# Trunk of a streaming encoder: sums of the first norm from two layouts of x, a 512-column first MLP product, and a written order for the last stage

## The chip, the cores and the metric

The kernel runs on one core of a Trainium2 chip. The time is that of one execution on the device, in microseconds, the median of several runs. The core has a matrix engine (PE; its weight loads are shown apart as PEld), a vector engine (DVE), a scalar engine (ACT), a third compute engine (POOL, also called GpSimd), and queues of DMA transfers, most of which are issued by SP. Each engine works through its own list of instructions in order and waits on semaphores where an operand comes from another engine.

## The reference, cut to what matters

With one layer (`DEPTH` is 1) the trunk is one Conformer convolution module, one squared-ReLU MLP and a final norm, on x of 512 tokens and 2048 channels in float32:

```python
h = rmsnorm(x, norm1_g)
u = h @ w_in + b_in                        # 2048 -> 2 * 2048
val, gate = split(u)
u = val * sigmoid(gate)
u = causal_dwconv(u, dw) + dw_b            # 31 taps for each channel
u = silu(layernorm(u, ln_g, ln_b))
x = x + u @ w_out + b_out
h = rmsnorm(x, norm2_g)
x = x + square(relu(h @ mlp_w1)) @ mlp_w2  # 2048 -> 8192 -> 2048
return rmsnorm(x, final_g)                 # rmsnorm: y * rsqrt(mean(y*y) + 1e-6) * g
```

## The kernel before, in words

Everything but the ends of the kernel lies channel-major: a tile holds 128 channels on the partitions and 512 tokens in the free dimension. To keep float32 precision each operand of a large product is split into a high part and a low rest, and each product is made of three matmuls (`mm3`, lines 377 to 382): weights-high by data-high, weights-high by data-low, weights-low by data-high. The high parts of weights are made on ACT (line 139, 237, 242), the low rests on POOL or DVE (line 140, 238, 243). A `Stream` object makes weight chunks some chunks ahead of their use (`AHEAD`), in four pairs of buffers.

The stages, in order of time:

- **Front.** 16 tiles of x arrive by DMA (`xt`). Each is multiplied by the norm's gain and split (`split_scaled`, ACT line 373, DVE line 374). Its squares are taken on ACT or DVE (string `SQ_X`) and added into two sums over channel tiles, `acc1` on POOL and `acc2` on DVE (string `ADD_X`, line 499); line 522 adds the two. `col_sums` (line 360) turns them into one number for each token by matmuls against ones, `inv_sqrt` makes the factor `r`, and `spread` (line 366) lays it out over the partitions as `row1`. The factor is applied only after the projection, so the matmuls of the input projection do not wait for it. The string `LO_W0` says which engine makes the low rests of the first eight weight chunks (v is DVE, g is POOL).
- **Input projection and convolution.** For each of 16 channel tiles j, 96 matmuls of 512 columns (`in_tile`) fill two PSUM banks. `gate(j)` and `glu(j)` make the gated value (DVE lines 411, 413, 421, ACT line 415), and `conv(j)` adds 31 taps, 24 or 25 of them on DVE (line 463), the others by ACT and POOL (lines 442, 452). The last tile is done in two halves, with some taps on PE by diagonal matrices (`diags`, line 566).
- **Layer norm and output projection** (line 758).
- **First MLP product.** The 64 tiles of 128 hidden channels are taken as 32 pairs. A pair's product is done by a Strassen-like scheme of seven products on halves (`FIRST`): halves of the input channels, of the pair, and of the tokens, so that each product has 256 columns (`HT`). A product is eight sets of `mm3`. Data tiles `y` hold high and low part side by side, 256 columns each. Four PSUM banks collect the products (`BANK`); P1, then P6, P7 and P4 accumulate in the same bank, and after each of these products the partial sum is read out into `four` (lines 1083, 1085, 1087). `Squares.step` then applies ReLU and square to the pair before, splits it and stores it to DRAM.
- **Second MLP product**, again in seven products, for all but the last two pairs of hidden tiles.
- **Last stage.** The last pair of hidden tiles is multiplied plainly for each block b of 128 tokens, in four pieces of 512 output columns (the last piece of the last block in two of 256). Each piece is added to the residual on DVE (`add`, line 1154), squared and summed on ACT (line 1230), multiplied by the final gain on POOL (line 1232; the block's last piece on DVE, line 1240), and, once all the block's sums are there, scaled by the norm's factor on ACT or DVE (lines 1247, 1249) and sent out by SP.

Inside `with tc.manual_schedule()` the instructions stand in each engine's list as the code writes them; elsewhere a scheduler of the tile library places them. Front, layer norm and both MLP products are written by hand; the pieces of the last stage are placed by the scheduler, all but the block of code around the norm's factor.

Of the kernel before, what the change touches and what calls it, by code (L numbers as in the profile page):

```python
# [12 lines left out]
F32 = mybir.dt.float32  # L13
# [5 lines left out]
P = 128  # L19
T = 512  # L20
# [26 lines left out]
ADD_X = "ggvgvgggggvgggvg"  # L47
SQ_X = "avaavaavaavaavaa"
LO_W0 = "vvvvgvgg"
# [34 lines left out]
def trunk(ctx: ExitStack, tc: tile.TileContext, xT, vec, fg, w_in, w_out, w1s, w2s, w2b, out):  # L84
# [272 lines left out]
    def col_sums(dst, acc):  # L357

        for b in range(NTOK):
            nc.tensor.matmul(out=dst[:, b : b + 1], lhsT=acc[:, b * P : (b + 1) * P], rhs=ones, start=True, stop=True)  # L360

# [129 lines left out]
    sums_on = [(nc.gpsimd, acc1) if c == "g" else (nc.vector, acc2) for c in ADD_X]  # L491
    with tc.manual_schedule():
        begun = set()
        pending = None

        def add(item):
            eng, acc, sq = item
            if sq is not acc:
                eng.tensor_tensor(out=acc, in0=acc, in1=sq, op=ALU.add)

        stream.AHEAD = 0
        for k in range(NT):
            nc.sync.dma_start(out=xt[k], in_=xT[:, k, :])
            if k % 4 == 1 and k > 1:
                stream.emit()
# [5 lines left out]
            eng, acc = sums_on[k]  # L511
            first = id(acc) not in begun
            begun.add(id(acc))
            sq = acc if first else early.tile([P, T], F32, tag="t", name="sq", bufs=4)
            if SQ_X[k] == "a":
                nc.scalar.activation(out=sq, in_=xt[k], func=AF.Square)
            else:
                nc.vector.tensor_tensor(out=sq, in0=xt[k], in1=xt[k], op=ALU.mult)
            pending = (eng, acc, sq)
        add(pending)  # L520
        if len(begun) > 1:
            nc.vector.tensor_tensor(out=acc1, in0=acc1, in1=acc2, op=ALU.add)
# [3 lines left out]
        for k in range(NT):  # L526
            in_tile(0, k, w0[k // 4])
            if k % 4 == 3:
                stream.emit()
        w1 = [chunk() for _ in range(4)]  # L530
        pvg[1] = (bank(), bank())
        st = bank("ax")
        col_sums(st, acc1)
        ms = tmp.tile([P, NTOK], F32, tag="st", name="ms")
        nc.vector.tensor_scalar(out=ms, in0=st[:, :NTOK], scalar1=1.0 / D, scalar2=None, op0=ALU.mult)
        r = inv_sqrt(ms, eps_rms, RMS_EPS, NTOK)
# [758 lines left out]
```

## Time and profile before

| | before |
|---|---|
| median of 3 runs | 1876.59 us (1876.09 to 1877.53) |
| the profiled execution | 1875.1 us, span of its instructions 1873.3 us |
| busy share | PE 98%, PEld 87%, DVE 67%, ACT 62%, POOL 68% |
| mean granted TensorE clock | 0.993 of full |

The span is the time from the first to the last instruction of the profiled execution. A busy share counts time in which at least one instruction of the engine runs. Matmuls are pipelined: a row gives the time from start to modelled end of one, and the distance between the starts of two rows is what one costs.

### The profile page before, as it was taken

The page shows a single profiled execution, that of the slowest core. Times are in us where ns is not written, and L with a number is a line of the kernel's source. Part 1 is how long each engine was busy: PE and PEld are TensorE (multiplying, and loading weights), DVE is VectorE, ACT ScalarE, POOL GpSimd, SP SyncE. Part 2 cuts the span into 40 slices and gives each one's busy share as a digit, 9 for nine tenths or more (in the row PEclk, how much of TensorE's full clock was granted, in tenths as well). Part 3 has the DMA queues.
Part 4 walks back from the last instruction along what each step waited for, and adds up shares of the span by engine and source line. Part 5 has one row for each costly group of instructions (what it writes and reads, how often), then busy time and mean ns, then how long its engine had stood idle before and what let it go on. Part 6 is the DMA issues. An engine that isn't in the chain of part 4 may idle for free.

```text
span 1873.3 us, 29336 instructions
## 1 busy us (share of the span) xinstructions
PE 1827.9 (98%) x10860; PEld 1629.8 (87%) x10860; DVE 1254.7 (67%) x2001; ACT 1157.0 (62%) x1782; POOL 1271.5 (68%) x718
## 2 busy tenths in 40 slices
PE   6999999989999999999999999999999999999996
PEld 4888888879888999999999999998888888888875
DVE  8899999994338655555555555545666666665676
ACT  6444444456337666666666666647777777777774
POOL 6689999954432676776776776766666677566654
PEclk9999999999999999999999999999999999999998
DMA  5233333206333465565565565586557456474332
GB/s 204 95 102 100 104 114 111 80 1 214 113 113 128 154 219 190 180 218 192 179 216 196 179 215 193 178 309 239 214 196 283 159 222 247 174 280 186 137 133 90
DMA packets 91439, 320.99 MB, mean 171 GB/s; under 512 B 10144, under 2 KB 11808, under 8 KB 91296
## 3 DMA queue, kind: packets, MB, share of 16 engines
q1 hardware_dynamic: 70416, 257.71, 39.4%
q10 hardware_dynamic: 20880, 61.42, 8.2%
q8 instruction: 85, 1.39, 0.3%
q14 instruction: 58, 0.48, 0.1%
HBM read 254.60 MB, written 64.49 MB: 170 GB/s over the span
## 4 chain that ended last, share of the span: by engine, by line
PE 83%; DVE 12%; ACT 2%; issue 1%; DMA 1%; ACTq 0%; SPq 0%; POOL 0%; DVEq 0%; POOLq 0%
PE mm L380 25%; PE mm L381 25%; PE mm L382 25%; PE mm L758 7%; DVE ax L463 4%; DMA xt<-in_xT 1%; DVE xl L374 1%; DVE d L647 1%; DVE u L421 0%; DVE y L893 0%; DVE d L725 0%; DVE acc L1154 0%; DVE wl L140 0%; PE ax L901 0%; DVE xr L915 0%
## 5 line engine op out<-in xcount | busy, mean ns | idle before, releaser
L380 PE MATMUL mm<-y,wh 128*128 128x256 f32 x1792 | 508.7, 284 | 2.0 <-ACT x L912 1.1
L381 PE MATMUL mm<-y,wh 128*128 128x256 f32 x1792 | 508.3, 284 | 1.7 <-DVE y L893 1.7
L382 PE MATMUL mm<-y,wl 128*128 128x256 f32 x1792 | 508.2, 284 | 0.0
L238 POOL TENSOR_TENSOR wl<-b,wh 128x1024 fp32r<-128x1024 f32 x96 | 231.6, 2412 | 215.0 <-ACT wh L237 215.0
L380 PEld LDWEIGHTS mm<-y,wh 128*128 128x128 f32 x1792 | 345.1, 193 | 2.4 <-ACT x L912 1.3
L381 PEld LDWEIGHTS mm<-y,wh 128*128 128x128 f32 x1792 | 345.2, 193 | 1.9 <-DVE y L893 1.9
L214 DVE TENSOR_TENSOR wl<-b,ax 128x512 fp32r<-128x512 f32 x360 | 231.4, 684 | 171.7 <-ACT ax L213 127.0
L382 PEld LDWEIGHTS mm<-y,wl 128*128 128x128 f32 x1792 | 345.1, 193 | 0.0
L380 PE MATMUL mm<-wh,ah 128*128 128x512 f32 x840 | 326.9, 389 | 1.2 <-DVE acc L1154 1.2
L381 PE MATMUL mm<-wl,ah 128*128 128x512 f32 x840 | 326.8, 389 | 0.0
L382 PE MATMUL mm<-wh,al 128*128 128x512 f32 x840 | 326.8, 389 | 0.0
L187 POOL TENSOR_TENSOR b<-b,b 128x1024 f32<-128x1024 f32 x120 | 286.8, 2413 | 47.9 <-DVE wl L214 33.9
L207 ACT CAST wh<-b 128x1024 fp32r<-128x1024 f32 x210 | 221.3, 1054 | 151.5 <-PE mm L382 150.8
L140 POOL TENSOR_TENSOR wl<-raw,wh 128x1024 fp32r<-128x1024 f32 x85 | 206.8, 2452 | 103.1 <-ACT wh L139 103.0
L463 DVE SCALAR_TENSOR_TENSOR ax<-u,v,ax 128x512 f32<-128x512 f32 x327 | 218.1, 750 | 0.0
L380 PE MATMUL mm<-xh,wh 128*128 128x512 f32 (+1 forms) x544 | 207.1, 381 | 5.7 <-ACT wh L139 5.2
L381 PE MATMUL mm<-xl,wh 128*128 128x512 f32 (+1 forms) x544 | 207.7, 382 | 3.2 <-DVE xl L374 3.0
L382 PE MATMUL mm<-xh,wl 128*128 128x512 f32 (+1 forms) x544 | 206.6, 380 | 2.9 <-DVE wl L140 2.9
L213 ACT COPY ax<-wh 128x512 f32<-128x512 f32 x360 | 199.8, 588 | 5.7
L1154 DVE SCALAR_TENSOR_TENSOR acc<-mm,shift,acc 128x512 f32<-128x512 f32 (+1 forms) x241 | 169.6, 743 | 31.6 <-PE mm L382 31.6
L380 PEld LDWEIGHTS mm<-wh,ah 128*128 128x128 f32 x840 | 157.7, 188 | 34.7 <-ACT w2h L1205 1.6
L382 PEld LDWEIGHTS mm<-wh,al 128*128 128x128 f32 x840 | 157.7, 188 | 32.7
(216 smaller groups left out, 3047.3 us busy)
## 6 DMA issues: line engine op xcount, KB each, us to landing
b<-in_w1s SPq DMA_DIRECT2D x128, 512.0 KB, 4.6
b<-in_w2s SPq DMA_DIRECT2D x120, 512.0 KB, 6.7
raw<-in_w_in SPq DMA_DIRECT2D x63, 512.0 KB, 3.3
ah<-spill SPq DMA_DIRECT2D x26, 896.0 KB, 8.7
al<-spill SPq DMA_DIRECT2D x26, 896.0 KB, 10.3
raw<-in_w_out SPq DMA_DIRECT2D x32, 512.0 KB, 3.3
spill<-sh ACTq DMA_DIRECT2D x31, 512.0 KB, 7.2
spill<-sl ACTq DMA_DIRECT2D x31, 512.0 KB, 5.9
```

The costliest lines, as they stand in the source:

```text
L140: (nc.vector if sl.stop == cut else self.eng).tensor_tensor(out=lo[:, sl], in0=raw[:, sl], in1=hi[:, sl].bitcast(F32), op=ALU.subtract)
L187: nc.gpsimd.tensor_tensor(out=raw[to, hs], in0=raw[x, hs], in1=raw[y, hs], op=ALU.subtract)
L207: nc.scalar.copy(out=hi, in_=self.s)
L213: nc.scalar.copy(out=st, in_=hi[:, sl].bitcast(F32))
L214: nc.vector.tensor_tensor(out=lo[:, sl], in0=self.s[:, sl], in1=st, op=ALU.subtract)
L238: nc.gpsimd.tensor_tensor(out=lo, in0=raw[b], in1=hi.bitcast(F32), op=ALU.subtract)
L380: nc.tensor.matmul(out=ps, lhsT=wh, rhs=xh, start=first, stop=False, **how)
L381: nc.tensor.matmul(out=ps, lhsT=wh, rhs=xl, start=False, stop=False, **how)
L382: nc.tensor.matmul(out=ps, lhsT=wl, rhs=xh, start=False, stop=last, **how)
L463: nc.vector.scalar_tensor_tensor(out=o, in0=a, scalar=w, in1=c, op0=ALU.mult, op1=ALU.add)
L758: nc.tensor.matmul(out=ps[n][:, sl], lhsT=a[:, wsl], rhs=x[:, sl], start=first and a is wh and x is hi, stop=last and x is lo)
L1154: nc.vector.scalar_tensor_tensor(out=t, in0=ps, scalar=r2[:, b : b + 1], in1=t, op0=ALU.mult, op1=ALU.add)
```

## The change

The squares of channels 0 to 1023 are still taken from the channel-major tiles (all on ACT), and are added on DVE, in a PSUM bank, with no work on POOL. Those of channels 1024 to 2047 come from a second, token-major copy of that half of x (`x2d`, four tiles of 128 tokens by 1024 channels, four added DMA transfers of 512 KB): one ACT instruction squares a tile and adds along the free dimension, so that the result is already one number for each token. The sums by matmul are now issued after k = 13 of the first projection tile, `spread` after k = 2 of the second, and a sigmoid on a dummy follows the square root on ACT. Two more low rests of the first weight chunks change engine or place, and the twelve activations that make `diags` move to a place after the last full convolution.

In the first MLP product weights-high is multiplied by the whole data tile, high and low part in one matmul of 512 columns, and weights-low by the high part, 256 columns. The two halves of the bank are added while they are read out: one instruction takes the first half, one more on DVE adds the second.

In the last stage all is written in order: block b's square root factor and scaled outputs stand between the pieces of block b + 1, and the gain of a block's last piece moves to POOL, but for the last block.

```diff
-ADD_X = "ggvgvgggggvgggvg"
-SQ_X = "avaavaavaavaavaa"
-LO_W0 = "vvvvgvgg"
+STAT_AT = 13
+ROW_AT = 3
+SQ_AT = (10, 12, 14, 15)
+SQ_DVE = ()
+LO_W0 = "vvvvvvgg"
...
+        def squares(b):
+            t = big.tile([P, 2 * T], F32, tag="rb", name="xs")
+            nc.sync.dma_start(out=t, in_=x2d[b])
...
+                nc.scalar.activation(out=t, in_=t, func=AF.Square, accum_out=ms[:, b : b + 1])
...
+            elif k % 4 == 3:
+                stream.emit()
             if pending:
-                add(pending)
...
+                nc.vector.tensor_tensor(out=pending[0], in0=sq_acc, in1=pending[1], op=ALU.add)
+                pending = None
+            if k == 0:
+                nc.scalar.activation(out=sq_acc, in_=xt[k], func=AF.Square)
+            elif k < NT // 2:
+                sq = early.tile([P, T], F32, tag="t", name="sq", bufs=4)
                 nc.scalar.activation(out=sq, in_=xt[k], func=AF.Square)
...
+                pending = (acc1 if k == NT // 2 - 1 else sq_acc, sq)
+            if k in SQ_AT:
+                squares(SQ_AT.index(k))
+        stream.emit()
...
+            if k == STAT_AT:
+                st = bank("ax")
+                for b in range(NTOK):
+                    nc.tensor.matmul(out=st[:, b : b + 1], lhsT=acc1[:, b * P : (b + 1) * P], rhs=ones, start=True, stop=True)
...
+        nc.scalar.activation(out=root0, in_=eps_rms, func=AF.Sigmoid)
...
-                nc.scalar.activation(out=self.a[:, HT:], in_=self.a[:, HT:], func=AF.Relu)
+                nc.scalar.activation(out=self.a, in_=self.a, func=AF.Relu)
...
                 for p in range(8):
                     t = y[p, product]
-                    sl = slice(p * P, (p + 1) * P)
-                    mm3(x, tuple(h[:, sl] for h in w), (t[:, :HT], t[:, HT:]), product in OPENS and p == 0, p == 7, skip_group_check=True)
+                    wh, wl = (h[:, p * P : (p + 1) * P] for h in w)
+                    nc.tensor.matmul(out=x, lhsT=wh, rhs=t, start=product in OPENS and p == 0, stop=p == 7, skip_group_check=True)
+                    nc.tensor.matmul(out=x[:, :HT], lhsT=wl, rhs=t[:, :HT], start=False, stop=p == 7, skip_group_check=True)
...
-                if product in ("P1", "P5", "P6"):
-                    nc.scalar.copy(out=to, in_=x)
-                elif product == "P4":
-                    nc.scalar.activation(out=to, in_=x, func=AF.Relu)
+                if product in ("P2", "P7", "P3"):
+                    nc.vector.tensor_tensor(out=to, in0=x[:, :HT], in1=to, op=ALU.add)
                 else:
-                    nc.vector.tensor_tensor(out=to, in0=x, in1=to, op=ALU.add)
+                    nc.scalar.copy(out=to, in_=x[:, :HT])
+                nc.vector.tensor_tensor(out=to, in0=x[:, HT:], in1=to, op=ALU.add)
...
+    with tc.manual_schedule():
+        before = None
+        for b in range(NTOK):
+            row = Row(b)
+            for i, cs in enumerate(row.cols):
+                row.piece(i, cs)
+                if before and i == 0:
+                    before.factor()
+                    before.scale(3, False)
+                    before.scale(2, False)
+                elif before and i < 3:
+                    before.scale(2 - i, True)
+                if i < len(row.cols) - 1:
+                    row.gain(i, nc.gpsimd)
+            row.total()
+            row.gain(i, nc.gpsimd if b < NTOK - 1 else nc.vector)
+            before = row
+        before.factor()
+        for i in (4, 0, 3, 1, 2):
+            before.scale(i, i < 2)
```

`Row.piece` holds a piece's matmuls, its `add` and its square; `total` the sum and square root, `factor` the three small DVE instructions behind it, `scale` the scaled output and its DMA.

**Engine PE, first MLP product, before** (`mm` is the PSUM bank, `y` the data tile with high and low part, `wh` and `wl` the high and low weights; the end of two sets and the start of a third):

```order
L380 MATMUL mm_5318<-y_4390,wh_8710 128x256
L381 MATMUL mm_5318<-y_4390,wh_8710 128x256
L382 MATMUL mm_5318<-y_4390,wl_8711 128x256
L380 MATMUL mm_5318<-y_4423,wh_8710 128x256
L381 MATMUL mm_5318<-y_4423,wh_8710 128x256
L382 MATMUL mm_5318<-y_4423,wl_8711 128x256
L380 MATMUL mm_5318<-y_4698,wh_8710 128x256
L381 MATMUL mm_5318<-y_4698,wh_8710 128x256
```

The same engine and stage in the change, the last sets of one product and the first of the next:

```order
L1082 MATMUL mm_5309<-y_5350,wh_7612 128x512
L1083 MATMUL mm_5309<-y_5350,wl_7613 128x256
L1082 MATMUL mm_5309<-y_5394,wh_7612 128x512
L1083 MATMUL mm_5309<-y_5394,wl_7613 128x256
L1082 MATMUL mm_5311<-y_4383,wh_7645 128x512
L1083 MATMUL mm_5311<-y_4383,wl_7646 128x256
```

Three matmuls of 256 columns on a data tile have become one of 512 and one of 256.

**Engine DVE, end of the front, before** (`xl` is the low part of an x tile, `sq` squares, `wl` low weights, `ms` the mean of squares; in brackets the engines or transfers waited for):

```order
L374 SCALAR_TENSOR_TENSOR xl_259<-xt13_122,v_91,xh_258 128x512 [waits DMAHW2_49,Activation_49]
L518 TENSOR_TENSOR sq_263<-xt13_122 128x512 [waits Pool_49]
L374 SCALAR_TENSOR_TENSOR xl_267<-xt14_123,v_91,xh_266 128x512 [waits DMAHW4_49,Activation_49]
L374 SCALAR_TENSOR_TENSOR xl_275<-xt15_124,v_91,xh_274 128x512 [waits DMAHW5_49,Activation_49]
L499 TENSOR_TENSOR acc2_108<-acc2_108,sq_271 128x512 [waits DVE_49]
L522 TENSOR_TENSOR acc1_107<-acc1_107,acc2_108 128x512 [waits DVE_49,Pool_49]
L140 TENSOR_TENSOR wl_341<-raw_342,wh_340 128x1024 [waits DMAHW0_49,PE_49,Activation_49]
L535 TENSOR_SCALAR ms_413<-ax_408 128x4 [waits PE_49]
```

The same engine and place in the change (`mq` is the sum of both parts of the mean of squares):

```order
L371 SCALAR_TENSOR_TENSOR xl_255<-xt13_122,v_91,xh_254 128x512 [waits DMAHW5_49,Activation_49]
L371 SCALAR_TENSOR_TENSOR xl_260<-xt14_123,v_91,xh_259 128x512 [waits DMAHW6_49,Activation_49]
L371 SCALAR_TENSOR_TENSOR xl_268<-xt15_124,v_91,xh_267 128x512 [waits DMAHW0_49,Activation_49]
L142 TENSOR_TENSOR wl_272<-raw_273,wh_271 128x1024 [waits DMAHW1_49,PE_49,Activation_49]
L142 TENSOR_TENSOR wl_281<-raw_282,wh_280 128x1024 [waits DMAHW3_49,PE_49,Activation_49]
L533 TENSOR_TENSOR mq_390<-ax_373,ms_132 128x4 [waits PE_49]
L534 TENSOR_SCALAR mq_390<-mq_390 128x4 [waits DVE_49]
```

The squares, the adds and the joint sum are gone from this end of the list, one more low rest stands before the sums, and no wait on POOL is left.

**Engine ACT, last block of tokens, before** (`acc` and two digits is the piece of block and column, `sq` its squares, `r4` the factor of a block; rows with `r4` scale an output):

```order
L1230 ACTIVATE sq_18790,ss_18781<-acc30_13394 128x512
L1247 ACTIVATE acc21_13434<-acc21_13434,r4_18762 128x512
L1247 ACTIVATE acc20_13385<-acc20_13385,r4_18762 128x512
L1230 ACTIVATE sq_18801,ss_18781<-acc31_13443 128x512
L1230 ACTIVATE sq_18812,ss_18781<-acc32_13497 128x512
L1230 ACTIVATE sq_18823,ss_18781<-acc33_13540 128x256
L1230 ACTIVATE sq_18834,ss_18781<-acc33_13540 128x256
L1238 ACTIVATE r1_18837<-r0_18836,eps_rms_61 128x1
```

The same engine and block in the change:

```order
L1238 ACTIVATE sq_17197,ss_17188<-acc30_11819 128x512
L1238 ACTIVATE sq_17215,ss_17188<-acc31_11868 128x512
L1260 ACTIVATE acc21_11859<-acc21_11859,r4_17183 128x512
L1238 ACTIVATE sq_17228,ss_17188<-acc32_11922 128x512
L1260 ACTIVATE acc20_11810<-acc20_11810,r4_17183 128x512
L1238 ACTIVATE sq_17241,ss_17188<-acc33_11965 128x256
L1238 ACTIVATE sq_17252,ss_17188<-acc33_11965 128x256
L1248 ACTIVATE r1_17255<-r0_17254,eps_rms_61 128x1
```

The two scaled outputs of block 2 have moved one square and two squares later, and now stand one by one between the squares of block 3.

## Rows read from the trace of the kernel before

**Rows 1.** The page's chain of work that ended last, shares of the span by engine.
```profile
PE 83%; DVE 12%; ACT 2%; issue 1%; DMA 1%; ACTq 0%; SPq 0%; POOL 0%; DVEq 0%; POOLq 0%
```

**Rows 2.** Busy time of each engine in stretches of the span: stretch, its length, busy us (instructions) of each engine, granted TensorE clock, share of the DMA engines, GB/s. The first two are the first 20 us of the front, the third is its end, the fourth lies in the input projection, the fifth in the first MLP product.
```profile
0.00:10.00 10.00, 4.26 (x9) 2.60 (x10) 3.77 (x12) 5.96 (x10) 0.70 (x6) 1.00 0.79 260
10.00:20.00 10.00, 7.37 (x29) 4.95 (x28) 10.00 (x9) 8.94 (x15) 7.19 (x4) 1.00 1.05 409
...
40.00:50.00 10.00, 5.67 (x24) 4.59 (x25) 6.80 (x8) 2.95 (x10) 6.74 (x3) 0.66 0.58 200
...
200.00:300.00 100.00, 100.00 (x443) 82.84 (x442) 97.31 (x138) 47.42 (x64) 92.49 (x55) 1.00 0.37 124
...
700.00:1300.00 600.00, 600.00 (x4775) 590.08 (x4775) 333.01 (x559) 384.67 (x610) 416.98 (x254) 1.00 0.60 211
```

**Rows 3.** Groups of instructions, shapes kept apart: line, engine, operation, tiles, output and input shape, count | busy us in all, mean ns of one | idle time before them.
```profile
L380 PE MATMUL mm<-y,wh 128*128 128x256 f32 x1792 | 508.7, 284 | 2.0 <-ACT x L912 1.1 <-ACT y L892 0.9
...
L1087 DVE TENSOR_TENSOR four<-mm,four 128x256 f32<-128x256 f32 x96 | 40.6, 423 | 7.4 <-PE mm L382 4.8
L1083 ACT COPY four<-mm 128x256 f32<-128x256 f32 x96 | 35.9, 374 | 87.4 <-PE mm L382 87.4
...
L1006 ACT ACTIVATE four<-four 128x1024 f32<-128x1024 f32 x32 | 34.0, 1062 | 0.0
```

**Rows 4.** Matmuls in order of time: start us, duration us, engine, line, operation. First two rows of the first MLP product with 55 more between them, then its last row and the first of the second product, then two rows of the last stage with 84 more between them and the first of 256 columns behind.
```profile
759.84 0.28 PE L380 MATMUL mm<-y,wh 128*128 128x256 f32 x1
...
766.56 0.28 PE L382 MATMUL mm<-y,wl 128*128 128x256 f32 x1
...
1242.12 0.28 PE L382 MATMUL mm<-y,wl 128*128 128x256 f32 x1
1242.24 0.40 PE L380 MATMUL mm<-wh,sh 128*128 128x512 f32 x1
...
1837.78 0.39 PE L381 MATMUL mm<-w2l,ah 128*128 128x512 f32 x1
...
1857.05 0.39 PE L382 MATMUL mm<-w2h,al 128*128 128x512 f32 x1
1857.28 0.28 PE L380 MATMUL mm<-w2h,ah 128*128 128x256 f32 x1
```

**Rows 5.** Matmuls of the front in order of time, with the idle time before them and what ended it: the first, the last of tile 0, the sums, the spread of the factor, and the next behind it.
```profile
5.24 0.79 PE L380 MATMUL mm<-xh,wh 128*128 128x512 f32 x1 [5.24 <-ACT wh L139]
...
38.10 0.39 PE L382 MATMUL mm<-xh,wl 128*128 128x512 f32 x1
41.28 1.05 PE L360 MATMUL ax<-ones,acc 128*128 128x1 f32 x8 [2.80 <-DVE acc L522]
...
47.28 2.07 PE L366 MATMUL ax<-ident,r 128*128 128x128 f32 x8 [3.05 <-DVE r L354]
49.01 0.77 PE L380 MATMUL mm<-xh,wh 128*128 128x512 f32 x1
```

**Rows 6.** DVE in the front, in order of time.
```profile
27.90 1.75 DVE L374 SCALAR_TENSOR_TENSOR xl<-xt,v,xh 128x512 fp32r<-128x512 f32 x1
...
31.28 0.74 DVE L374 SCALAR_TENSOR_TENSOR xl<-xt,v,xh 128x512 fp32r<-128x512 f32 x1
31.94 1.21 DVE L140 TENSOR_TENSOR wl<-raw,wh 128x1024 fp32r<-128x1024 f32 x1
...
44.46 0.15 DVE L535 TENSOR_SCALAR ms<-ax 128x4 f32<-128x4 f32 x1
...
45.07 1.70 DVE L349 TENSOR_SCALAR ve<-ms 128x4 f32<-128x4 f32 x1
...
47.07 0.16 DVE L354 SCALAR_TENSOR_TENSOR r<-yy,y 128x4 f32<-128x4 f32 x1
...
52.83 0.75 DVE L421 SCALAR_TENSOR_TENSOR u<-tv,v,sig 128x512 f32<-128x512 f32 x1 [1.53 <-ACT sig L415]
```

**Rows 7.** ACT in the front, in order of time.
```profile
4.17 0.72 ACT L373 ACTIVATE xh<-xt,v 128x512 fp32r<-128x512 f32 x1 [1.49 <-DMA v<-in_vec]
...
14.41 0.61 ACT L516 ACTIVATE sq<-xt 128x512 f32<-128x512 f32 x1
14.93 1.32 ACT L373 ACTIVATE xh<-xt,v 128x512 fp32r<-128x512 f32 x2
16.15 0.61 ACT L516 ACTIVATE sq<-xt 128x512 f32<-128x512 f32 x1
16.67 1.03 ACT L139 CAST wh<-raw 128x1024 fp32r<-128x1024 f32 x1
```

**Rows 8.** What DVE waited for between 60 and 380 us: us in total, times, longest.
```profile
DVE tg L411 <- PE mm L382: 4.7, 6, 1.7
```

**Rows 9.** The last stage, in order of time: the sums of blocks 2 and 3 on DVE, ACT between them, the last matmul, and the first of the last scaled outputs.
```profile
1857.72 0.16 DVE L1237 TENSOR_REDUCE r<-ss 128x1 f32<-128x4 f32 x1 [0.54 <-ACT sq L1230]
...
1864.71 0.16 DVE L1237 TENSOR_REDUCE r<-ss 128x1 f32<-128x5 f32 x1 [2.30 <-ACT sq L1230]
...
1864.97 1.14 DVE L1240 TENSOR_TENSOR acc<-acc,fgt 128x256 f32<-128x256 f32 x1
...
1861.32 1.33 ACT L1247 ACTIVATE acc<-acc,r 128x512 f32<-128x512 f32 x2 [2.50 <-DVE r L1243]
...
1858.59 0.28 PE L382 MATMUL mm<-w2h,al 128*128 128x256 f32 x1
```

More of the change, by code (lines that the diff above doesn't have):

```diff
@@ L490, in trunk @@
     make_identity(nc, ident)
-    sums_on = [(nc.gpsimd, acc1) if c == "g" else (nc.vector, acc2) for c in ADD_X]
     with tc.manual_schedule():
-        begun = set()
-        pending = None
[L496 to L501, printed above, removed]
+        stream.AHEAD = 0
+        sq_acc = bank("ax")
+        ms = tmp.tile([P, NTOK], F32, tag="st", name="ms")
+        def squares(b):
+            t = big.tile([P, 2 * T], F32, tag="rb", name="xs")
+            nc.sync.dma_start(out=t, in_=x2d[b])
+            if b in SQ_DVE:
+                nc.vector.tensor_tensor(out=t, in0=t, in1=t, op=ALU.mult)
+                nc.vector.tensor_reduce(out=ms[:, b : b + 1], in_=t, axis=mybir.AxisListType.X, op=ALU.add)
+            else:
+                nc.scalar.activation(out=t, in_=t, func=AF.Square, accum_out=ms[:, b : b + 1])
+        pending = None
         for k in range(NT):
             nc.sync.dma_start(out=xt[k], in_=xT[:, k, :])
-            if k % 4 == 1 and k > 1:
-                stream.emit()
             h[k] = split_scaled(xt[k], col(V_G1, k), "x")
@@ L527, in trunk @@
             in_tile(0, k, w0[k // 4])
-            if k % 4 == 3:
-                stream.emit()
+            if k == STAT_AT:
+                st = bank("ax")
+                for b in range(NTOK):
+                    nc.tensor.matmul(out=st[:, b : b + 1], lhsT=acc1[:, b * P : (b + 1) * P], rhs=ones, start=True, stop=True)
+        mq = tmp.tile([P, NTOK], F32, tag="st", name="mq")
+        nc.vector.tensor_tensor(out=mq, in0=st[:, :NTOK], in1=ms, op=ALU.add)
+        nc.vector.tensor_scalar(out=mq, in0=mq, scalar1=1.0 / D, scalar2=None, op0=ALU.mult)
+        r = inv_sqrt(mq, eps_rms, RMS_EPS, NTOK)
+        for _ in range(2):
+            stream.emit()
+        nc.scalar.activation(out=root0, in_=eps_rms, func=AF.Sigmoid)
         w1 = [chunk() for _ in range(4)]
         pvg[1] = (bank(), bank())
[L532 to L536, printed above, removed]
-        in_tile(1, 0, w1[0])
-        row1 = fore.tile([P, T], F32, tag="row", name="row1", bufs=2)
-        nc.scalar.copy(out=row1, in_=spread(r))
-        for k in range(1, NT):
+        for k in range(NT):
+            if k == ROW_AT:
+                row1 = fore.tile([P, T], F32, tag="row", name="row1", bufs=2)
+                nc.scalar.copy(out=row1, in_=spread(r))
             in_tile(1, k, w1[k // 4])
@@ L771, in trunk @@
         run(c14)
+        for n in range(max(PE_TAPS)):
+            w = V_DW + NT * KC - 1 - n
+            nc.scalar.activation(out=diags[:, n, :], in_=ident, func=AF.Copy, scale=v[:, w : w + 1])
         for c in range(4):
@@ new lines, in factor, with scale @@
+        def factor(self):
+            y, ve = self.y, self.ve
+            nc.vector.reciprocal(out=y, in_=self.root)
+            nc.vector.scalar_tensor_tensor(out=ve, in0=y, scalar=ve, in1=y, op0=ALU.mult, op1=ALU.mult)
+            nc.vector.scalar_tensor_tensor(out=self.r, in0=ve, scalar=1.5, in1=y, op0=ALU.add, op1=ALU.mult)
+        def scale(self, i, on_act):
+            x3, cs, _ = self.xs[i]
+            if on_act:
+                nc.scalar.activation(out=x3, in_=x3, func=AF.Copy, scale=self.r)
+            else:
+                nc.vector.tensor_scalar(out=x3, in0=x3, scalar1=self.r, scalar2=None, op0=ALU.mult)
+            nc.sync.dma_start(out=out[self.b * P : (self.b + 1) * P, cs], in_=x3)
```

69 lines of the change are left out of this document (22 added, 47 removed).

## The prediction, made before the changed kernel had run

> **What bounds the kernel now.** I read the chain of waits first: 83% of it is PE, 12% DVE, 2% ACT, and nothing else counts [rows 1]. Then the stretches, to see where PE is not the limit. The reader is to see three things there: from 700 to 1300 us PE is busy all of the time while DVE (333 of 600), ACT (385) and POOL (417) have room; from 200 to 300 us PE is at 100 but DVE at 97 and POOL at 92, so three engines end together; and in the front PE is not full while DVE is busy 10.00 of 10 us [rows 2]. So a gain in the first MLP product must come from PE's own time, a gain in the front is worth what it still is worth when the convolution has ended, and the last stage is read by its last wait.
>
> **Term A, the first MLP product.** What is paid here is the distance between starts of matmuls. With 256 columns, 56 distances from 759.84 to 766.56 us make 6.72 / 56 = 0.1200 us; with 512 columns, 85 distances from 1837.78 to 1857.05 make 19.27 / 85 = 0.2267 us [rows 4]. The 256 more columns cost 106.7 ns, which is 2.4 GHz, so both forms carry 120.0 - 106.7 = 13.3 ns that does not depend on the columns. The change makes of 256 + 256 + 256 columns 512 + 256: the same columns, one matmul less. A set cost 3 x 120.0 = 360.0 ns and will cost 226.7 + 120.0 = 346.7. Mixed neighbours occur twice: 256 to 512 starts are 0.12 apart, 512 to 256 0.23 [rows 4], so a matmul's distance follows its own size. There are 1792 sets, by the count of line 380 [rows 3]: 1792 x 13.3 ns = 23.9 us; a pair goes from 56 x 0.360 = 20.16 to 19.41 us, a product of eight sets takes 2.77.
>
> What is added lies beside PE. Each of seven products per pair gets one more DVE instruction of the kind of line 1087, 0.423 us [rows 3]: 2.96 us in a pair. DVE has 333 / 600 x 20.16 = 11.2 us in a pair now [rows 2] and would have 14.2 of 19.4; ACT has 12.9, and the ReLU widened from 768 to 1024 (1.06 us is what the 1024-wide ACT row of line 1006 takes [rows 3]) adds at most 0.3; POOL stays at 14.0. All have room, so the throughput price is nothing. The wait that could appear is at the bank that P1, P6, P7 and P4 share in turn: the readout of one (copy 0.374 plus add 0.423 [rows 3], some 0.8 to 1.3 us behind the product's end) must be done before the bank is opened again, at least one product of 2.77 us later by the order of products; the slack is some 1.5 us. What stands before the added instruction on DVE's list are the splits of data tiles of about the same length, one or two of which fit. I take off 1 us for the first pair, whose data tiles are still being made: its first matmul now needs the low part too, which before was needed one matmul later. A = 22.9, bounds 21 and 24.5.
>
> The Trainium skill (TensorE: Matmul & The Clock Gate, section "Back-to-back issue gap") gives the isolated distance of a warm matmul as columns over 2.4 GHz plus about 2.5 ns. By it one matmul less would save 2.5 ns x 1792 = 4.5 us, and A would be 4.5, not 23.9. The trace does not agree: 120.0 ns at 256 columns instead of 109.2, and 226.7 at 512 instead of 215.8; the measurement decides.
>
> **Term B, the front.** Before, the last matmul of tile 0 begins at 38.10. PE then waits 2.80 us for the joined sum, and after the sums 3.05 for r, and the next tile goes on at 49.01 [rows 5]; the granted clock of 40 to 50 us is 0.66 [rows 2], and the first matmul behind the spread lasts 0.77 instead of 0.39 [rows 5]. Tile 1 has 90 matmuls left there: 49.01 + 90 x 0.2267 + 2.5 (an estimate for the cold ones) = 71.9 us.
>
> After, the adds on POOL, the squares and the joint sum on DVE and their waits are gone, as the order of DVE shows. DVE's own rows tell why that speeds it: a low rest takes 1.75 us at 27.90, while at 31.28 it takes 0.74 with 0.66 to the next row [rows 6]; I put the long ones down to POOL running beside it. DVE then does 0.66 a tile and ACT becomes the feeder. Its list from 4.17 [rows 7]: 16 high parts at 0.66 = 10.6; 8 squares at 0.52 (14.41 to 14.93) = 4.2; four casts of 1.03 = 4.1; of the four token-major squares three stand before the last high part, at 1.06 (as the 1024-wide row of line 1006) = 3.2; 1.5 for transfers that come late, as long as its first wait. Sum 23.6, so the last high part is there at 27.8 and the last low rest at 28.6. PE alone would need 5.24 + 96 x 0.2267 = 27.0 and 1.05 for the sums. I take 31 for the end of tile 0. The transfers: on SP's queue three of the four added loads of 0.52 MB stand ahead of the last x tile, which makes 7.9 MB up to there (16 tiles of 0.26, 2.1 of weights, 1.6). The queues moved 2.6 MB in the first 10 us and 4.1 in the next [rows 2]; at 409 GB/s the other 1.2 MB are there at 23 us, before ACT comes to them.
>
> The sums are done inside tile 0. Behind them: the last cast on ACT, the two instructions on `mq`, and the chain to r, which took 47.23 - 44.46 = 2.8 with a 1.70 us row of POOL's neighbourhood in it [rows 6]; I take 2 and have r at 33.7. The spread stands after k = 2 of tile 1, that is at 31.9 + 18 x 0.2267 = 36.0: no wait left, the clock stays at 1.00. Spread 1 us, then tile 1's remaining 78 matmuls: 37 + 17.7 = 54.8, against 71.9: PE gains 17. DVE's convolution hangs on the first u, at 52.83 before [rows 6]. After: row1 at 37.7, the gate's own instructions, a cast in front of the sigmoid on ACT that itself waits for a matmul of tile 1 (k = 3, done at 38.4 or soon after), the sigmoid, u at 40.2: DVE gains 12.6.
>
> What survives to 380 us lies between the two. DVE waited for PE 4.7 us in all between 60 and 380 [rows 8]; with PE 17 ahead these waits go, so DVE can make up 12.6 + 4.7 = 17.3. PE cannot end the convolution without DVE. I take 16.5, nearer to PE's gain, since PE is the one with no idle time there [rows 2]. The twelve activations moved behind the last full convolution are at most 0.61 each as the 512-wide row [rows 7], 7 us on an ACT that is 47% busy there [rows 2]: nothing, and the same if they were all late, as they are needed by the last tile alone. Bounds of B: 12.5 and 17.3; 8 if ACT feeds 4 to 5 us later than added up.
>
> **Term C, the last stage.** The last matmul starts at 1858.59, but the sum of the last block is taken only at 1864.71, after DVE has waited 2.30 for ACT's squares [rows 9]. From the sum of block 2 at 1857.72 that is 7.0 us: ACT holds it, with scaled outputs (1.33 for two) between squares, and these wait 2.50 for the factor of block 2. The change puts the factor's DVE steps after piece 0 and the two ACT outputs one by one behind squares 1 and 2, as the order of ACT shows. The same instructions remain on ACT, five squares and two outputs; what can go is part of the wait. I take 0.7 for it, 0.6 for the last gain (1.14 at 256 columns [rows 9], where no POOL works beside it), 0.6 for the last outputs on two engines: C = 1.9. From above, if nothing but PE held it: an add of 0.42 [rows 3] and a square of at most 0.61 [rows 7] behind PE's end at 1858.9 put the sum at 1860, C = 4.7. From below, the written order makes an engine wait where a scheduler had filled in: -1.
>
> **Sum.** 22.9 + 16.5 + 1.9 = 41.3. The profiled execution took 1875.1, so 1833.8; it stands 1.5 under the median of the runs, 1876.59, so I say 1835. The bounds: 24.5 + 17.3 + 4.7 = 46.5 gives 1830, 21 + 8 - 1 = 28 gives 1849.
>
> **Rivals.**
> 1. *The distance of matmuls is not saved.* If a 512-column matmul in a stream that alternates with 256 costs as two of 256 (0.240), because each weight load stands out behind the short one, A is nearly nothing: 1858. For it: in the first MLP product weight loads are busy 590 of 600 us [rows 2]. Against it: they are hidden already at 0.120 a matmul, and the mixed neighbours in [rows 4] keep their own distances. 7%. By the distance that the Trainium skill states in the section named above, the time would be 1853.
> 2. *The front gains less*, because ACT, now with all squares, feeds PE 4 to 8 us later than summed: B = 8 to 12, time 1840 to 1844. For it: ACT was already busy 8.94 of the 10 us from 10 to 20 [rows 2], before anything is added; against: by the sum above it is done soon after PE's own minimum. 10%.
> 3. *Slower, by the shared bank.* Three times in a pair a product opens a bank whose content has just been read; with two instructions on two engines instead of one, DVE's is late whenever longer work stands in front. 32 x 3 = 96 hand-overs; each costs what the readout ends beyond 2.77 us after the product. With DVE 2 us behind at a product's end it begins to decide; at 0.43 us of wait each (96 x 0.43 = 41) it eats all the gains, and at 0.65 the time is 1897. For it: DVE goes from 11.2 to 14.2 us in a pair. Against: ACT stood idle 87.4 us for PE ahead of line 1083 and DVE 7.4 ahead of line 1087 [rows 3], so the readers are mostly ready first. 3%.
> That the change does not do what it says can be in the tail alone, since the order fixes the rest: C = 0 costs 2 us, inside the range.
>
> **How the numbers follow.** The forecast has 80%; its own range is 1830 to 1842. Rival 2 lies beside it, rival 1 above 1850 outside. The range 1829 to 1849 takes in the bounds and leaves out rivals 1 and 3 and some of the rest. A run of this kernel can tell 0.2%, 3.8 us, from no change. Forecast and rivals 1 and 2 are all faster, save a small part of 1 that meets other losses: faster 0.95, same 0.02, slower 0.03.
>
> **What would show it.** Step A: matmul starts 0.227 and 0.120 apart in turn, 19.4 us for a pair, no wait of PE for `four`. Step B: tile 0 ends at 31, no PE wait for sums or r, clock 1.00 from 40 to 50, first u near 40, and the convolution's end 16 us earlier. Step C: 6 to 7 us from the sum of block 2 to that of block 3. Wrong it would be if PE showed waits on line 1082 at the first set of P6, P7 or P4, if 512-column matmuls there lay 0.24 apart, or if DVE's waits for PE stayed in the convolution while u came early.

## The result and the profile after

The changed kernel took 1848.46 us in the median (4 executions: 1841.32, 1844.31, 1852.62, 1855.06), the kernel before beside it 1876.34; the ratio is 0.9851 with a 95% interval of 0.9808 to 0.9895. That is 27.9 us less, 0.7% above the predicted 1835 and within 1829 to 1849. The four executions of the kernel before lie within 3 us; those of the changed one spread over 14. The profiled execution is the fastest of the four.

Where its time went, stage by stage (starts in us; the rows stand below, or ahead of the prediction):

| | before | after | ahead |
|---|---|---|---|
| first u of the convolution | 52.83 | 39.25 | 13.6 |
| last tap on DVE | 409.12 | 395.84 | 13.3 |
| first MLP product begins | 588.30 | 576.23 | 12.1 |
| second product begins | 1242.24 | 1207.08 | 35.2 |
| last matmul | 1858.59 | 1823.40 | 35.2 |
| end of the span | 1873.3 | 1839.5 | 33.8 |

So 12.1 come from the front, 23.1 from the first product (653.9 us before, 630.9 after), and the last stage gives 1.4 back.

The stretches that answer to [rows 2], of the changed kernel:

```profile
40.00:50.00 10.00, 10.00 (x45) 8.26 (x44) 9.96 (x14) 5.46 (x8) 7.85 (x6) 1.00 0.21 65
200.00:300.00 100.00, 100.00 (x442) 82.79 (x442) 99.35 (x143) 45.48 (x60) 94.38 (x57) 1.00 0.33 104
700.00:1300.00 600.00, 600.00 (x3337) 524.03 (x3336) 421.07 (x765) 407.58 (x628) 430.10 (x257) 1.00 0.61 211
```

The stretch at 40 us with a granted clock of 0.66 is gone (1.00 now), DVE is busy 99 of 100 us in the convolution (97 before), and in the first product DVE took on 88 us in 600 (421 against 333) while PE stayed full.

Matmuls of the front, answering to [rows 5]:

```profile
5.34 0.80 PE L377 MATMUL mm<-xh,wh 128*128 128x512 f32 x1 [5.34 <-ACT wh L141]
...
27.50 0.95 PE L531 MATMUL ax<-ones,acc 128*128 128x1 f32 x8
...
31.17 0.39 PE L377 MATMUL mm<-xh,wh 128*128 128x512 f32 x1
...
35.25 1.05 PE L363 MATMUL ax<-ident,r 128*128 128x128 f32 x8
...
53.86 0.39 PE L377 MATMUL mm<-xh,wh 128*128 128x512 f32 x1
```

No row has a wait but the first. Tile 1 begins at 31.17 and tile 2 at 53.86: the prediction said 31 and 54.8.

Groups of the first product, answering to [rows 3]:

```profile
L1082 PE MATMUL mm<-y,wh 128*128 128x512 f32 x1792 | 623.5, 392 | 5.1 <-DVE y L896 2.9 <-DVE four L1091 1.2 <-ACT x L915 1.0
...
L1091 DVE TENSOR_TENSOR four<-mm,four 128x256 f32<-128x256 f32 x224 | 95.1, 424 | 90.6 <-ACT four L1090 87.4
```

PE lost 5.1 us in 1792 sets, 1.2 of them to the readout (`four`), all in the first two pairs. DVE waits 87.4 us for ACT's copy; beyond those 1.2 us no PE matmul waits for DVE's added readout.

The last stage, DVE, from the sum of block 2 to that of block 3, answering to [rows 9]:

```profile
1824.54 0.16 DVE L1247 TENSOR_REDUCE r<-ss 128x1 f32<-128x4 f32 x1 [1.93 <-ACT sq L1238]
...
1826.20 1.89 DVE L1262 TENSOR_SCALAR acc<-acc,r 128x512 f32<-128x512 f32 x2
1828.01 2.18 DVE L1158 SCALAR_TENSOR_TENSOR acc<-mm,shift,acc 128x512 f32<-128x512 f32 x4
1832.17 0.16 DVE L1247 TENSOR_REDUCE r<-ss 128x1 f32<-128x5 f32 x1 [1.98 <-ACT sq L1238]
```

From sum to sum it takes 7.6 us now, 7.0 before. Two scaled outputs take 1.89 and stand ahead of the next adds, on which ACT's squares wait. The sum of block 2 already comes 1.1 us behind the start of the last matmul (1823.40); before it came 0.9 ahead of it (1857.72 and 1858.59). So the earlier blocks had grown longer too: from the sum of block 0 to that of block 3 it takes 23.3 us, before 20.2.

### The profile page after: what moved, and what is told of

Same layout as the page of the kernel before. It is cut to its first block, busy times and chain, and to the rows that moved or that the text cites. A ratio compares the mean times of both kernels' runs of the same rounds, so it can differ in the third digit from the quotient of the medians.

```text
span 1839.5 us, 25968 instructions
## 1 busy us (share of the span) xinstructions
PE 1802.6 (98%) x9068; PEld 1534.2 (83%) x9068; DVE 1329.8 (72%) x2222; ACT 1169.4 (64%) x1788; POOL 1251.5 (68%) x709
## 4 chain that ended last, share of the span: by engine, by line
PE 81%; DVE 14%; ACT 3%; issue 1%; DMA 0%; ACTq 0%; DVEq 0%
PE mm L1082 21%; PE mm L377 14%; PE mm L378 14%; PE mm L379 14%; PE mm L1083 11%; PE mm L758 7%; DVE ax L460 7%; DVE u L418 1%; DVE d L647 1%; DVE ol L563 0%; DVE ax L456 0%; DVE acc L1158 0%; DVE y L896 0%; ACT sq L1238 0%; DVE ax L462 0%
## 5 line engine op out<-in xcount | busy, mean ns | idle before, releaser
L1082 PE MATMUL mm<-y,wh 128*128 128x512 f32 x1792 | 623.5, 392 | 5.1 <-DVE y L896 2.9
L1083 PE MATMUL mm<-y,wl 128*128 128x256 f32 x1792 | 502.2, 280 | 0.0
L1082 PEld LDWEIGHTS mm<-y,wh 128*128 128x128 f32 x1792 | 335.7, 187 | 79.8 <-DVE y L896 3.2
L1083 PEld LDWEIGHTS mm<-y,wl 128*128 128x128 f32 x1792 | 339.2, 189 | 0.0
L378 PEld LDWEIGHTS mm<-wl,ah 128*128 128x128 f32 x840 | 157.7, 188 | 32.6
L141 ACT CAST wh<-raw 128x1024 fp32r<-128x1024 f32 (+1 forms) x91 | 93.8, 1038 | 140.9 <-PE mm L378 92.4
```

Source lines behind the costliest of these rows:

```text
L378: nc.tensor.matmul(out=ps, lhsT=wh, rhs=xl, start=False, stop=False, **how)
L1082: nc.tensor.matmul(out=x, lhsT=wh, rhs=t, start=product in OPENS and p == 0, stop=p == 7, skip_group_check=True)
L1083: nc.tensor.matmul(out=x[:, :HT], lhsT=wl, rhs=t[:, :HT], start=False, stop=p == 7, skip_group_check=True)
```

## The experiments

**The parts by themselves.** Each kernel takes the sections of the diff for one stage into the kernel before, and nothing else; the fourth is the change again.

```diff
 # first: the hunks of the first MLP product alone
+nc.tensor.matmul(out=x, lhsT=wh, rhs=t, ...)
 # second: the hunks of the front alone
+nc.scalar.activation(out=t, in_=t, func=AF.Square, accum_out=ms[:, b : b + 1])
 # third: the hunks of the last stage alone
+class Row:
```

> The kernel before with the first MLP product of the change and nothing else. Theory (a matmul's distance is columns at 2.4 GHz plus 13.3 ns, and the added readout hides): 23 us faster than before, about 1853, all executions within 2 us of each other. Rival (the shared bank or the third, wider readout costs time in some executions): the four-way spread of the change, some 14 us from fastest to slowest, shows here too, and the mean gain is well under 23.

Measured: 1853.3, 1863.72, 1864.53, 1865.29, 1866.64, 1866.79 us; ratio 0.9933 (0.9913 to 0.9953). The theory failed in five of six executions, which gain 9 to 12 us instead of 23; the rival's spread is here, but not by its cause, as the traces below show no wait.

> The kernel before with the front of the change alone (token-major half of the sums, sums inside tile 0, diagonals placed later). Theory: in the profiled execution of the change PE stood 17.8 us ahead at the end of the input projection and 12 to 13.5 at the start of the first MLP product, so 12 to 14 us faster, 1862 to 1864; if the spread of the change comes from here, single executions lie from 1862 to 1876. Rival: the spread comes from another part, and all executions lie within 2 us.

Measured: 1863.91 (1863.16 to 1865.94), ratio 0.9938 (0.9926 to 0.995): 11.6 us, and no spread.

> The kernel before with the written order of the last stage alone. By the profiled execution of the change, where the last matmul starts 35.2 us earlier but the span is only 33.8 shorter, it loses 1 to 1.5 us: 1877.5 to 1878. The prediction's term said 1.9 us faster, 1874.5. If the spread of the change came from the tail, executions would differ by up to 14 us here.

Measured: 1876.53 against 1875.53, ratio 1.0004 (0.9996 to 1.0013): the written order gains nothing, and a loss of 1 us can't be told from none here.

> The change itself, a second time, for its spread and a second trace. If the parts add, its fastest is near 1841 (23 + 13 - 1.4 under 1876), and a slow execution shows in a stretch of its trace where the time was lost; if the first four times were an accident of that chip, all lie within 2 us.

Measured: 1841.76, 1852.34, 1853.49, 1854.82, 1855.76; ratio 0.9885 (0.987 to 0.9899). The parts add, and of nine executions of the change in all, three lie at 1841 to 1844 and six at 1852 to 1856. These five ran on one chip, so the chip alone does not choose.

None of the six was profiled; a trace of the longer kind exists of the product alone. Matmuls in order of time, start and duration: first the change, profiled in 1841.32 us, a set of one pair and the same place 29 pairs later, and the end of the stage.

```profile
624.68 0.39 PE L1082 MATMUL mm<-y,wh 128*128 128x512 f32 x1
624.91 0.28 PE L1083 MATMUL mm<-y,wl 128*128 128x256 f32 x1
...
1187.67 0.39 PE L1082 MATMUL mm<-y,wh 128*128 128x512 f32 x1
...
1207.08 0.39 PE L377 MATMUL mm<-wh,sh 128*128 128x512 f32 x1
```

The same places in the product alone, profiled in 1863.72 us:

```profile
588.60 0.39 PE L1079 MATMUL mm<-y,wh 128*128 128x512 f32 x1
...
637.47 0.40 PE L1079 MATMUL mm<-y,wh 128*128 128x512 f32 x1
637.71 0.28 PE L1080 MATMUL mm<-y,wl 128*128 128x256 f32 x1
...
699.65 0.40 PE L1079 MATMUL mm<-y,wh 128*128 128x512 f32 x1
...
700.01 0.40 PE L1079 MATMUL mm<-y,wh 128*128 128x512 f32 x1
...
700.36 0.40 PE L1079 MATMUL mm<-y,wh 128*128 128x512 f32 x1
...
700.71 0.40 PE L1079 MATMUL mm<-y,wh 128*128 128x512 f32 x1
...
1211.28 0.40 PE L1079 MATMUL mm<-y,wh 128*128 128x512 f32 x1
...
1231.07 0.40 PE L380 MATMUL mm<-wh,sh 128*128 128x512 f32 x1
```

29 pairs take 562.99 us in one and 573.81 in the other: 19.41 and 19.79 for a pair, with no wait in either. A pair has 56 sets, so a set takes 346.7 or 353.3 ns, and the 6.7 ns between them are 12.0 us in 1792 sets. Neither is a stall: from the third pair on, all pairs of a trace agree to 0.02 us. Nor is it the granted clock, which is 1.00 from 700 to 1300 us in both. In the shorter spacing every set is alike; in the longer one sets of 0.36, 0.35 and 0.35 us follow each other in turn (the four starts at 700 us). That the six longer executions of the change have this spacing is an inference from their 12 us. In the second trace of the change the spacing changes within one execution. The starts of four products:

```profile
605.34 0.40 PE L1082 MATMUL mm<-y,wh 128*128 128x512 f32 x1
...
608.17 0.40 PE L1082 MATMUL mm<-y,wh 128*128 128x512 f32 x1
...
616.80 0.39 PE L1082 MATMUL mm<-y,wh 128*128 128x512 f32 x1
...
619.57 0.39 PE L1082 MATMUL mm<-y,wh 128*128 128x512 f32 x1
```

Eight sets take 2.83 us ahead of an uneven stretch at 611 to 614 us, and 2.77 behind it and to the end.

**One matmul's fixed cost.** Only the joint matmul is undone, the readouts stay. (Both halves open the bank's sum. The Trainium skill, PSUM — Partial Sum Buffer, section "The four PSUM rules", says that an opening matmul clears the marks of the whole bank; no row of a trace here shows these marks. By that rule this kernel leaves the opening set's part of the first half out of the sums. The instructions are as many and as large as meant.)

```diff
-nc.tensor.matmul(out=x, lhsT=wh, rhs=t, ...)
+nc.tensor.matmul(out=x[:, :HT], lhsT=wh, rhs=t[:, :HT], ...)
+nc.tensor.matmul(out=x[:, HT:], lhsT=wh, rhs=t[:, HT:], ...)
```

> The change, but each 512-column matmul of the first MLP product split again into two of 256 on the two halves of the bank; both readout instructions stay. Theory (the gain of the product is one matmul's fixed 13.3 ns per set, and the added readouts hide): a pair takes 20.16 us again, the whole 1863 to 1866 (the front alone gave 1863.9), and all executions lie within 3 us, since the two spacings of the change (19.41 or 19.79 us a pair) belong to the mixed stream. Rival (the added readouts cost something): a pair takes longer than 20.16 and the time is above 1867.

Measured: 1865.33 (1864.88 to 1866.76). First matmul of the stage, and the first behind it:

```profile
577.73 0.28 PE L1083 MATMUL mm<-y,wh 128*128 128x256 f32 x1
...
1231.77 0.40 PE L377 MATMUL mm<-wh,sh 128*128 128x512 f32 x1
```

654.0 us, as the 653.9 before: at this pace the 224 added readouts cost nothing, and the whole gain is the saved matmul. (At the pace of the change PE waited 1.2 us for them, as said above.)

**Fewer changes of size.**

```diff
 # grouped: all wide matmuls of a product first
+for p, (wh, t) in enumerate(wide):
     nc.tensor.matmul(out=x, lhsT=wh, rhs=t, ...)
+for p, (_, t) in enumerate(wide):
     nc.tensor.matmul(out=x[:, :HT], lhsT=wl, rhs=t[:, :HT], ...)
 # alternating: 512, 256, 256, 512, ...
+if p % 2: the 256-column matmul first
```

> The change, but within a product all eight 512-column matmuls come first and then all eight of 256. Theory (executions fall apart because 512 and 256 alternate: the distance behind a 512-column matmul is 0.2300 us in a fast and 0.2367 in a slow one, fixed when PE last stood still): no alternation, so every execution has 19.4 us a pair and the time is 1840 to 1844 in all of them. Rival (the slow spacing comes from the bank's readout, the data or the chip): executions still fall into two groups some 12 us apart, 1842 and 1854.

Measured: 1845.89, 1845.91, 1845.93, 1847.91, ratio 0.9849 (0.9835 to 0.9862). One group, as expected, but not the expected 1840 to 1844: all four lie above the change's three at 1841 to 1844, and the stage takes 635.2 us, against 630.9 at 19.41 us a pair.

> The change, with the two matmuls of every second set in the other order (512, 256, 256, 512, ...), so that sizes change half as often. If the slow spacing comes from the change of size, 6.7 ns at each, the slow executions come 6 us sooner than those of the change (1847 instead of 1853) or do not occur. Rival (it comes from 512-column matmuls as such): executions again at 1842 and 1853.

Measured: 1844.97 to 1846.89 in five executions, ratio 0.9838 (0.9824 to 0.9851); the stage, first matmul to first of the next:

```profile
577.43 0.39 PE L1084 MATMUL mm<-y,wh 128*128 128x512 f32 x1
...
1211.18 0.40 PE L377 MATMUL mm<-wh,sh 128*128 128x512 f32 x1
```

633.8 us, no second group. Neither order shows the spread: they lie 1 to 7 us above the change's three shorter executions and 4 to 11 below its six longer ones. So each order pays a part of the difference every time. Each round of runs had a chip of its own, and the change was not executed again in these two, so a part of the chip in it isn't excluded; the kernel at the end, with the second order, ran on yet another chip and has no spread either.

**Why the front keeps 12 of 16.5.** In these rows `tg` is the gate's part with the norm's factor, `sig` its sigmoid, `u` the gated value, `wh` high weights. DVE's waits between 40 and 380 us in the change, the longest; then the same wait before:

```profile
DVE u L418 <- ACT sig L412: 7.5, 9, 2.0
```

```profile
DVE u L421 <- ACT sig L415: 2.1, 4, 1.5
```

No wait of `tg` for PE is left, as predicted (4.7 us before), but `u` waits for the sigmoid, 7.5 us against 2.1 before. ACT and DVE at the end of tile 3:

```profile
103.69 1.05 ACT L141 CAST wh<-raw 128x1024 fp32r<-128x1024 f32 x1 [4.38 <-PE mm L378]
104.65 0.72 ACT L412 ACTIVATE sig<-tg,v 128x512 f32<-128x512 f32 x1
```

```profile
101.55 0.67 DVE L408 TENSOR_TENSOR tg<-row,mm 128x512 f32<-128x512 f32 x1
...
105.40 2.37 DVE L418 SCALAR_TENSOR_TENSOR u<-tv,v,sig 128x512 f32<-128x512 f32 x1 [1.98 <-ACT sig L412]
```

The sigmoid's operand is there at 102.2, but ahead of it in ACT's list stands a weight cast for a later tile, which waits 4.38 us for PE to free its buffer. So DVE still goes at PE's pace. Two tries to move the sigmoid ahead:

```diff
 # first: the whole loop in written order, AHEAD 3
+with tc.manual_schedule():
 # second: one order more, the cast behind the sigmoid
+tc.add_manual_dep(cast, sigmoid, NoSync)
```

> The kernel before with the front of the change, and the convolution loop in written order, so that on ACT the sigmoid of a tile stands behind only those weight casts that wait for earlier chunks. Theory (in the change DVE keeps only its own 13.3 us because the sigmoid stands behind a cast that waits for PE: 7.5 us of waits of u for the sigmoid in place of the 4.7 for PE): those waits fall under 2 us, the last tap comes 3 to 6 us earlier than in the front alone (397.5), and the time is 1858 to 1861. Rival (POOL at 94% or PE is the bound instead): the last tap and the time stay within 1 us of the front alone (1863.9), or PE starts to wait for low rests.

Measured: 1899.99 (1898.34 to 1900.81). It tells nothing on the sigmoid: the written order made new waits, among them PE's for the first tile's mean (`ax`) and ACT's for transfers, and those of `u` grew to 25.7 us.

```profile
ACT wh L141 <- DMA raw<-in_w_in: 43.8, 4, 13.5
DVE u L418 <- ACT sig L412: 25.7, 14, 12.2
...
PE ax L471 <- DVE d L465: 16.4, 1, 16.4
```

> The kernel before with the front of the change, and one order more on ACT: the last of the four weight casts that stood ahead of a tile's sigmoid comes behind it. Theory (DVE's waits for PE of 4.7 us came back as waits of u for the sigmoid of 7.5 us, because the sigmoid stands behind a cast that waits for PE): these waits fall under 3 us, the last tap of the last half tile comes 4 us or more earlier than in the front alone (397.5, after a first u at 41.2), the whole 1858 to 1861. Rival (POOL, 94% busy, or DVE's own list is the bound in any case): waits of u for the sigmoid go, but others take their place; last tap and time within 1 us of the front alone, 1863.9.

Measured: 1859.44 (1858.42 to 1860.8), ratio 0.9909 (0.9895 to 0.9922) against 0.9938 for the front alone. DVE's waits between 40 and 380 us, then its first u and last tap:

```profile
DVE u L418 <- ACT sig L412: 1.6, 4, 1.0
DVE tg L408 <- PE mm L379: 1.3, 2, 0.7
```

```profile
40.05 2.37 DVE L418 SCALAR_TENSOR_TENSOR u<-tv,v,sig 128x512 f32<-128x512 f32 x1 [1.00 <-ACT sig L412]
...
391.89 0.48 DVE L649 SCALAR_TENSOR_TENSOR ax<-u,v,ax 128x256 f32<-128x256 f32 x1
```

From first u to last tap 351.8 us, against 356.6 in the change and 356.3 before: one cast moved in each tile is worth 4.8 us there. The front as a whole is then worth 16.5 by the medians (1875.91 - 1859.44) and 14.5 in the traces, where the first MLP product begins at 573.81 instead of 588.30.

**The diagonals.** Their twelve activations back in the old place:

```diff
 diags = fore.tile(...)
+for n in range(max(PE_TAPS)): nc.scalar.activation(out=diags[:, n, :], ...)
```

> The kernel before with the front of the change, but the twelve activations that make the diagonals back in their old place. In the change PE waits 2.30 us for the first of them. Theory (that wait is covered, since the next matmuls wait for POOL's sums of the tile before anyway): within 0.5 us of the front alone, 1863.9. Rival (it is on the path): about 2 us faster, 1862.

Measured: 1864.88 (1864.57 to 1867.31), ratio 0.9951 (0.9939 to 0.9964): no faster, perhaps 1 or 2 us slower than the front alone. The wait of 2.2 us for the first diagonal goes, and one of 3.8 for POOL's sums takes its place (waits of PE, 340 to 400 us):

```profile
PE mm L664 <- POOL acc L480: 3.8, 1, 3.8
```

**The last stage.** Sum, factor and outputs one or two pieces later in the lists:

```diff
 if before and i == 0:
+    before.total()
+elif before and i == 1:
     before.factor()
     before.scale(3, False)
```

> The kernel before with the written last stage, each block's sum, factor and scaled outputs one to two pieces later in the list: the sum behind the add of the next block's piece 0, the factor and a scaled output behind that of piece 1, and so on. Theory (the written order gains nothing because DVE waits for ACT's squares ahead of every sum and does two slowed scaled outputs, 1.9 us, ahead of the next adds): block 3's sum comes within 4 us of the last matmul's start, against 6.1 before and 8.8 in the written order, and the whole is 2 to 4 us faster than before, 1871 to 1873. Rival (POOL's gains or the scaled outputs themselves set the pace, whatever their places): no faster than the written order, 1875 to 1877.

Measured: 1876.29 against 1875.91, ratio 1.0002 (0.9993 to 1.0011): the rival. DVE, and POOL beside it:

```profile
1860.28 0.16 DVE L1249 RECIPROCAL r<-r 128x1 f32<-128x1 f32 x1 [0.41 <-ACT r L1244]
1860.48 0.96 DVE L1250 SCALAR_TENSOR_TENSOR r<-r,r 128x1 f32<-128x1 f32 x1
1861.47 1.18 DVE L1251 SCALAR_TENSOR_TENSOR r<-r,r 128x1 f32<-128x1 f32 x1
...
1867.51 0.22 DVE L1250 SCALAR_TENSOR_TENSOR r<-r,r 128x1 f32<-128x1 f32 x1
1867.77 0.16 DVE L1251 SCALAR_TENSOR_TENSOR r<-r,r 128x1 f32<-128x1 f32 x1
```

```profile
1860.17 1.25 POOL L1239 TENSOR_TENSOR acc<-acc,fgt 128x512 f32<-128x512 f32 x1
1861.39 1.25 POOL L1239 TENSOR_TENSOR acc<-acc,fgt 128x512 f32<-128x512 f32 x1
```

Two instructions on one number a partition take 2.14 us beside the last two of POOL's four gains in a row, and 0.38 behind the last block, where POOL is idle. Each ends where a gain ends: 1861.44 and 1861.42, 1862.65 and 1862.64. So each of the two waits for one gain of POOL, however small it is itself; the reciprocal ahead of them, also beside a gain, takes its 0.16. The Trainium skill (Advanced Engine Details and Errata, section "Mode Summary") says that DVE's second port to SBUF is shared with GpSimd, so that GpSimd instructions and DVE instructions in a 2-port mode block each other. The trace agrees that they block; whether these two run in such a mode no row shows.

**All of it together**, with POOL's share of the gains halved by scaling and multiplying in one DVE instruction:

```diff
-nc.vector.tensor_scalar(out=x3, in0=x3, scalar1=self.r, ...)
+nc.vector.scalar_tensor_tensor(out=x3, in0=x3, scalar=self.r, in1=g, ...)
```

> The change with three edits together: alternating order of the two matmuls in a set, a weight cast behind the sigmoid, and in the last stage the later places of sum, factor and outputs, where now the two outputs that DVE scales take the final gain in the same instruction, so that POOL multiplies two pieces of a block instead of four. If the parts add: 1875.9 before, less 16.5 (front with the sigmoid's order) and 20.2 (first MLP product at 633.8 instead of 653.9 us) is 1839. Theory on the last stage (POOL's gains slow DVE: small instructions of 0.16 us took 1.0 to 1.2 beside them, and two outputs 1.9): with half of them gone the stage is 3 to 5 us shorter, 1834 to 1836. Rival (the chain from square to square on ACT sets the stage whatever POOL does): 1838 to 1840.

Measured: 1840.64 (1839.12 to 1841.67), ratio 0.9816 (0.9802 to 0.9829): all five executions lie at 1839 to 1842, where only the two fastest of the change's nine lie. The front and the first product add to within 2 us (1839 reckoned); the last stage, from the last matmul's start at 1823.29 to the end at 1839.7, is no shorter than in the change. The time is near the rival's, but its reason is not shown: ACT still waits for DVE's adds, and POOL's remaining gains still stand beside the factor:

```profile
1818.27 2.54 POOL L1248 TENSOR_TENSOR acc<-acc,fgt 128x512 f32<-128x512 f32 x2 [4.59 <-ACT sq L1243]
```

```profile
1818.61 0.97 DVE L1259 SCALAR_TENSOR_TENSOR r<-r,r 128x1 f32<-128x1 f32 x1
1819.62 1.22 DVE L1260 SCALAR_TENSOR_TENSOR r<-r,r 128x1 f32<-128x1 f32 x1
```

## Why the prediction was right, and where it was not

- **Term A** (22.9): right in mechanism; 23.1 in the profiled execution. The size holds in three executions of nine only. The step that failed is "Mixed neighbours occur twice ... so a matmul's distance follows its own size": two single distances, read to 10 ns, could not show 6.7 ns. Where a set takes 353.3 ns, as in the traced execution of the product alone, half of the 13.3 ns is lost, and A is 11.5 (653.94 less 642.47); the times of the other six of nine say the same. Rival 1 had the right place with twice the price, and the sign named for it, 512-column matmuls 0.24 apart, shows in that trace. The added readouts were free but for 1.2 us, about as said, and rival 3 fell with them.
- **Term B** (16.5): its start came out to within 1 us (tile 1 at 31.2, spread at 35.3, first u at 39.3 where 31, 36.0 and 40.2 were said). The step that failed is "with PE 17 ahead these waits go, so DVE can make up 12.6 + 4.7": the waits for PE came back as waits for a sigmoid behind a cast that waits for PE. The front was worth 12.1 in the trace and 11.6 alone, below the lowest value named for the likeliest case (12.5). The prediction had named such a cast for the first u and not asked for it in the tiles behind. With one cast a tile moved the front gives 14.5 in the traces and 16.5 by the medians, so the way of counting holds once these waits are gone. The price of the diagonals, nothing, held.
- **Term C** (1.9): no gain; 1.4 lost in the trace, 1.0 alone (with an interval that includes no change). The step that failed is "the same instructions remain ... what can go is part of the wait": the sum comes 8.8 us behind the last matmul's start instead of 6.1. In the order of the rows two outputs, 0.87 before and 1.89 beside POOL's gains, now stand ahead of the adds; that they are the cause is argued, not shown, since the two later tries changed the order and POOL's share without a gain. The last outputs became 1.3 us shorter (8.6 to 7.3 from sum to end), a little more than the 1.2 reckoned for them and the last gain.
- **Sum.** 41.3 said, 33.8 in the profiled execution, 27.9 in the median: of the 13.4 missing, 4.4 are B, 3.3 C, and the rest the two spacings of A. All three errors went the same way.
- **Luck.** The median of 1848.46 lies within 1829 to 1849 because two of those four executions are of the shorter kind (1841.32 and 1844.31). The five executions of the second time have their median at 1853.49, outside the range. The range reaches down to that gain by a weak front and last stage; what came was half of term A missing, which no bound of A (21 to 24.5) allows for.

## What to carry to other kernels

A wait that disappears from one engine must be looked for on the next in the chain: read the in-order list of the engine that delivers the operand, and ask what each instruction ahead of it waits for. A saving of a few ns for each of thousands of matmuls has to be measured over hundreds of them in the very mix that will run, and in several executions. A gain on POOL beside small DVE instructions is not free for DVE: 0.96 and 1.18 us in place of 0.22 and 0.16.

## What was not expected of the hardware

A stream that alternates 512- and 256-column matmuls keeps one of two spacings, 346.7 or 353.3 ns a set on the mean, for nearly a whole stage of 630 us. In the shorter all sets are alike, in the longer three unlike sets repeat. By the times, the choice differs from execution to execution of one program. One trace shows it change once, at an uneven stretch of the second pair, and the nine executions of the two orders in which sizes change less often lie within 3 us. What chooses it stays open: no run set it on purpose.

A DVE instruction on a single number a partition can wait for a whole gain of POOL: in eight places, four in the kernel with the later places and four in the last one, it ends within 0.02 us of the end of one. The wait lasted up to 1.2 us.
